# A transformer block on one core: the last down projection gets its weight remainders from adding transfers, and two more seven-product steps

## The chip, the cores and the metric

The kernel runs on one core of a Trainium2 chip, in one launch. The metric is the device time of a run in microseconds; for the kernel before it is the median of three runs. Beside it stands one profiled execution, whose trace gives start, duration and waits of every instruction.

## The reference

The reference is one block of a network with 256 rows (tokens) of width 2048, in float32: a first feed-forward part, a mixer of attention and convolution, and a second feed-forward part. Each reads the modulated norm of `x` and adds its gated result to `x`. The change concerns the last product of the second feed-forward part:

```python
def swiglu(h, w_gu, w_down):
    gu = jnp.einsum('bsd,df->bsf', h, w_gu)
    g, u = jnp.split(gu, 2, axis=-1)
    return jnp.einsum('bsf,fd->bsd', jax.nn.silu(g) * u, w_down)
...
h = modulate(rms_norm(x, ffn2_norm[l]), sh2, sc2)
x = x + FFN_RESIDUAL_WEIGHT * g2[:, None, :] * swiglu(h, ffn2_w_gu[l], ffn2_w_down[l])
```

Here `silu(g) * u` has 256 rows and 5632 columns, and `w_down` is 5632 x 2048.

## The kernel before, in words

**Split products.** TensorE multiplies in a rounded format (`F32R`). To keep float32's accuracy, each operand is split into its rounded part ("hi") and the remainder of the rounding ("lo"), and each product is made of three matmuls into one accumulator: hi by hi (L329), hi of the activations by lo of the weights (L333), and lo of the activations by hi of the weights (L334). This is `mm3`. The three are issued in this order; the second is the first to read a weight's remainder.

**Tiles of weights.** A weight tile is 1 MB, 128 partitions x 4 blocks of 512 columns. `w_tile` loads it from SP's queue into a buffer "raw" (L294; four buffers for the whole kernel), and for each half of it (two blocks, 128 x 1024) ScalarE casts the half to "whi" (L305; four buffers) and VectorE subtracts the cast from the raw half into "wlo" (L307; four buffers). The modulation's tiles (`w_ada`) also use "raw" buffers, but none is left after the first step of the stage below.

**The last down projection** is `down_strassen` (some 228 us at the end of the kernel). It makes the 2048 output columns in two pairs of 1024 (`np_` 0 and 1). In a pair it runs over 22 tiles (`c`), each of which holds 256 rows of `w_down` by 1024 columns, as a two by two matrix of blocks; the activations of the step are two by two as well (two halves of the 256 rows of `x`, two halves of the 256 contraction rows). Four accumulators `plain` hold the four output blocks. There are two kinds of steps:

- The ordinary step takes eight products (24 matmuls): for each half of the contraction and each output block, one product into that block's accumulator. Its tile comes from `w_tile`.
- The seven-product step, for the `c` in `SEVENS[np_]`, is a Strassen-Winograd step: 21 matmuls, on blocks, on sums of activation blocks and on differences of weight blocks, into `plain` and into four further accumulators `seven`, which are added to the outputs at the end of the pair. It loads "raw" (L542), casts and subtracts four groups (`split`, L512 and L513: b11, then b21 and b22, then t1 and t3, then t4 and t2), and makes the differences in place in "raw" on VectorE (L547, L549, L550). The sums of activations come from `sums_of` (L485 to L503: six operations on VectorE and a cast on ScalarE); those of the first `KEPT` = 6 seven-product steps of the first pair are kept for the second.

So a seven-product step takes four "whi" and four "wlo" buffers, an ordinary step two of each. Tiles 20 and 21 of the second pair are "held": their products are made last, output block by output block, so that each block can be finished and stored while the next is made.

**Order.** The kernel is written as a plain sequence; a scheduler places each engine's instructions in its queue, by their order in the program and by when it expects their operands, and adds the waits on data and on buffers that come free. An engine works through its queue in order.

Of the kernel before, what the change touches and what calls it, by code (L numbers as in the profile page):

```python
# [16 lines left out]
F32 = mybir.dt.float32  # L17
F32R = mybir.dt.float32r
# [4 lines left out]
ALU = mybir.AluOpType  # L23
AX = mybir.AxisListType

P = 128
# [27 lines left out]
TAPS_OUT = 12  # L54
WIDE = tuple(range(CK - 9, CK - 1))

SEVENS = ((3, 5, 9, 11, 13, 15, 17), (1, 3, 5, 7, 9, 11, 13, 15, 17))
KEPT = 6
CROSSBAR = {0: False, 96: True}
RMS_EPS = 1e-6  # L60
# [22 lines left out]
def block_kernel(ctx: ExitStack, tc: tile.TileContext, x_in, pos_in, w_ada, small, w_gu1, w_dn1,  # L83
                 w_in, w_out, w_gu2, w_dn2, out):
    nc = tc.nc
# [3 lines left out]
    rawp = ctx.enter_context(tc.tile_pool(name="rawp", bufs=4))  # L89
    whp = ctx.enter_context(tc.tile_pool(name="whp", bufs=4))  # L90
# [9 lines left out]
    def nm(s):  # L100
        uid[0] += 1
        return f"{s}_{uid[0]}"

    def blk(shape, dtype=F32):
        return blkp.tile(shape, dtype, tag="blk", name=nm("blk"))
# [38 lines left out]
    for i in range(4):  # L144
        pc = acc_tile()
        for j in range(4):
            k = 4 * i + j
# [138 lines left out]
    w_dma = [None]  # L286

    def w_tile(src, held=False, ks=(0, 4), small_raw=False):

        k0, n = ks[0], ks[1] - ks[0]  # L290
        src = src.rearrange("p (k n) -> p k n", k=4)
        if not small_raw:
            raw = rawp.tile([P, 4, 512], F32, tag="raw", name=nm("raw"))
            w_dma[0] = nc.sync.dma_start(out=raw[:, :n, :], in_=src[:, k0:k0 + n, :])  # L294
        views = {}
        for h in range(0, n, 2):
            m = min(2, n - h)
            if small_raw:
                part = blk([P, 2, 512])
                w_dma[0] = nc.sync.dma_start(out=part[:, :m, :], in_=src[:, k0 + h:k0 + h + m, :])  # L300
                rw = part[:, :m, :]
            else:
                rw = raw[:, h:h + m, :]
            hi = blk([P, 2, 512], F32R) if held else whp.tile([P, 2, 512], F32R, tag="whi", name=nm("whi"))
            nc.scalar.copy(out=hi[:, :m, :], in_=rw)  # L305
            lo = blk([P, 2, 512], F32R) if held else wlp.tile([P, 2, 512], F32R, tag="wlo", name=nm("wlo"))
            nc.vector.tensor_sub(out=lo[:, :m, :], in0=rw, in1=hi[:, :m, :].bitcast(F32))  # L307
            for j in range(m):
                views[k0 + h + j] = (hi[:, j, :], lo[:, j, :])
        return lambda j: views[j]  # L310

    def w_first(cs, held):
# [152 lines left out]
    def down_strassen(w_dn, aT, a_act, gate_of, evac_last, share, pend, finish):  # L465
# [13 lines left out]
        def sums_of(c):  # L479

            if c in kept:
                return kept[c]
            a = aT[c]
            full = tmp([P, 2, S])
            nc.vector.tensor_add(out=full, in0=a[:, 0].bitcast(F32), in1=a[:, 1].bitcast(F32))  # L485
            a11, a21, a12, a22 = full[:, 0, :P], full[:, 0, P:], full[:, 1, :P], full[:, 1, P:]
            q = tmp([P, 4, P])
            nc.vector.tensor_add(out=q[:, 0], in0=a21, in1=a22)
            nc.vector.tensor_sub(out=q[:, 1], in0=q[:, 0], in1=a11)
            nc.vector.tensor_sub(out=q[:, 2], in0=a11, in1=a21)  # L490
            nc.vector.tensor_sub(out=q[:, 3], in0=a12, in1=q[:, 1])
            keep = c in SEVENS[0][:KEPT]
            i = len(kept)
            if keep:
                if i < 2:
                    sp = in_c_bc[:, i]
                else:
                    sp = blk([P, 2, 4, P], F32R)
                hi, lo = sp[:, 0], sp[:, 1]
            else:  # L500
                hi, lo = tmp([P, 4, P], F32R), tmp([P, 4, P], F32R)
            nc.scalar.copy(out=hi, in_=q)
            nc.vector.tensor_sub(out=lo, in0=q, in1=hi.bitcast(F32))  # L503
            res = [(hi[:, i], lo[:, i]) for i in range(4)]
            if keep:
                kept[c] = res
            return res

        def split(src, n):
            hi = whp.tile([P, 2, 512], F32R, tag="whi", name=nm("whi"))  # L510
            lo = wlp.tile([P, 2, 512], F32R, tag="wlo", name=nm("wlo"))
            nc.scalar.copy(out=hi[:, :n, :], in_=src)  # L512
            nc.vector.tensor_sub(out=lo[:, :n, :], in0=src, in1=hi[:, :n, :].bitcast(F32))  # L513
            return [(hi[:, i, :], lo[:, i, :]) for i in range(n)]
# [4 lines left out]
        for np_ in range(2):  # L519
# [17 lines left out]
            for c in range(NCH):  # L537
                share()
                first, last = c == 0, c == NCH - 1
                if c in SEVENS[np_]:  # L540
                    raw = rawp.tile([P, 4, 512], F32, tag="raw", name=nm("raw"))
                    nc.sync.dma_start(out=raw, in_=w_dn[np_, c].rearrange("p (k n) -> p k n", k=4))  # L542
                    s1, s2, s3, s4 = sums_of(c)
                    (b11,) = split(raw[:, 0:1, :], 1)
                    b21, b22 = split(raw[:, 2:4, :], 2)

                    nc.vector.tensor_sub(out=raw[:, 0:2, :], in0=raw[:, 1:4:2, :], in1=raw[:, 0:2, :])  # L547
                    t1, t3 = split(raw[:, 0:2, :], 2)
                    nc.vector.tensor_sub(out=raw[:, 3, :], in0=raw[:, 3, :], in1=raw[:, 0, :])  # L549
                    nc.vector.tensor_sub(out=raw[:, 2, :], in0=raw[:, 2, :], in1=raw[:, 3, :])  # L550
                    t4, t2 = split(raw[:, 2:4, :], 2)
                    go, end = c == SEVENS[np_][0], c == SEVENS[np_][-1]
                    if go:
                        if np_ == 0:
                            seven = [acc_tile(), acc_tile(), tp_tile(), tp_tile()]
                        else:
                            seven = [acc_tile() for _ in range(4)]
                    mm3(seven[0], a_act(2 * c, 0), b11, go, end)
                    mm3(plain[0], a_act(2 * c + 1, 0), b21, False, False)
                    mm3(plain[1], s4, b22, False, False)  # L560
                    mm3(seven[1], s1, t1, go, end)
                    mm3(seven[3], s3, t3, go, end)
                    mm3(seven[2], s2, t2, go, end)
                    mm3(plain[2], a_act(2 * c + 1, 1), t4, False, False)
                    tick()
                    if end:

                        p1, p5, p6, p7 = seven
                        u = [tmp([P, 512]) for _ in range(5)]
                        last_pair = np_ == 1  # L570
                        nc.scalar.copy(out=u[0], in_=p1)
                        nc.vector.tensor_add(out=u[4], in0=p6, in1=u[0])

                        def step_1(u=u, p5=p5):
                            nc.vector.tensor_add(out=u[1], in0=p5, in1=u[4])

                        def step_2(u=u, p7=p7):
                            nc.vector.tensor_add(out=u[2], in0=p7, in1=u[4])

                        def step_3(u=u, p5=p5):  # L580
                            nc.vector.tensor_add(out=u[3], in0=p5, in1=u[2])

                        def add(i, u=u):

                            t, n, xs = place(i)
                            nc.vector.tensor_mul(out=u[i], in0=u[i], in1=gbc[n])
                            nc.vector.tensor_add(out=xs, in0=xs, in1=u[i])

                        if last_pair:
                            todo += [lambda: (step_1(), add(0), add(1)), lambda: (step_2(), step_3(), add(2)),  # L590
                                     lambda: add(3)]
                        else:
                            todo += [step_1, step_2, step_3]
                    continue
                w = w_tile(w_dn[np_, c])
                if np_ == 1 and c >= NCH - 2:
                    held.append((c, w))
                    if todo:
                        todo.pop(0)()
                    continue  # L600
                for k in range(2):
                    for i, (t, n) in enumerate(order):
                        mm3(plain[i], a_act(2 * c + k, t), w(2 * k + n), first and k == 0, last and k == 1)
                tick()
                if first and np_ == 0:
                    while pend:
                        finish(*pend.pop(0))
                    gbc = gate_of()
                if todo:
                    todo.pop(0)()  # L610
# [691 lines left out]
    for ci in range(10):  # L1302
        p0 = 1 if ci < HOLD else 0
        accs = first[ci][2] if ci < HOLD else [acc_tile() for _ in range(NT)]
        for pc in range(p0, 4):
# [3 lines left out]
            w = w_tile(w_in[ci, pc], ci == 0 and pc <= PRE)  # L1309
# [52 lines left out]
    for i, (n, pc) in enumerate([(n, pc) for pc in range(4) for n in range(3)]):  # L1362
        w = w_tile(w_out[n, pc])
# [106 lines left out]
```

## Time and profile before

| | |
|---|---|
| median of 3 runs | 1831.31 us (1829.83 to 1831.4) |
| the profiled execution | 1830.85 us, span of its trace 1829.0 us |
| mean granted TensorE clock | 0.998 |
| TensorE busy | 1800.7 us (98%) |
| VectorE busy | 1531.0 us (84%) |
| ScalarE busy | 1010.5 us (55%) |
| GpSimd busy | 28.3 us (2%) |
| read from DRAM | 492.37 MB, 270 GB/s over the span |
| queues of transfers | all data on SP's hardware queue |

How to read the profile's rows: PE is TensorE's matmuls, PEld its weight loads, DVE VectorE, ACT ScalarE, POOL GpSimd, SPq the queue from which SP issues transfers. In a group's row, "L307 DVE TENSOR_TENSOR wlo<-raw,whi 128x1024 ... x50 | 59.5, 1218 | 5.5 <-ACT whi L305 5.5" is the line, the engine, the operation, what it writes and reads, the count, then the busy time in us and the mean of one in ns, then how long the engine stood idle just before these instructions and what ended that idle time. In a row in order of time the first two numbers are start and duration in us; a matmul's duration overlaps the next one's. In a table of stretches stand the length, then for each engine the busy time and the count of instructions, then the granted clock of TensorE, the busy share of the transfer engines and what they moved. A transfer's row ends with the median time from its issue to its landing. A row of waits names who waited for whom, and then the sum, the times and the longest, in us.

### The profile page before, as it was taken

To read this page: it belongs to the slowest core of one execution; us is meant where nothing else is said; L and a number is where in the kernel's file an instruction comes from. 1 tells how busy PE (TensorE), PEld (TensorE's weight loads), DVE (VectorE), ACT (ScalarE), POOL (GpSimd) and SP (SyncE) were. 2 spreads that over 40 slices of the span, in tenths; PEclk is the share of its full clock that TensorE was granted. 3 is DMA by queue.
4 is the path that set the end of the run, shared out by engine and by line. 5 is a ranking of instruction groups with operands and counts; after the bars stand their busy time and mean duration, and the time that the engine had idled before them with its cause. 6 is when DMAs were issued, how large, how long until landed. Compare 5 with 4: busy or idle time off the path is not lost.

```text
span 1829.0 us, 21917 instructions
## 1 busy us (share of the span) xinstructions
PE 1800.7 (98%) x8111; PEld 1480.9 (81%) x8111; DVE 1531.0 (84%) x2040; ACT 1010.5 (55%) x1527; POOL 28.3 (2%) x29
## 2 busy tenths in 40 slices
PE   6999999999999999999999999999999999999998
PEld 5788888888888887788888787888888888878787
DVE  7889869999888787898999778878887865599897
ACT  7554344444444343566798655664755665555453
POOL 0000000000000000000110100000000000000000
PEclk9999999999999999999999999999999999999999
DMA  9987978889889998775544466889898966655552
GB/s 375 359 308 296 349 276 300 336 314 339 338 325 352 352 340 331 285 262 198 184 142 158 174 240 254 324 338 347 278 300 289 328 232 202 218 200 221 184 213 110
DMA packets 95962, 501.68 MB, mean 274 GB/s; under 512 B 31424, under 2 KB 31856, under 8 KB 38384
## 3 DMA queue, kind: packets, MB, share of 16 engines
q1 hardware_dynamic: 95856, 500.30, 74.7%
q8 instruction: 63, 1.03, 0.2%
q14 instruction: 43, 0.35, 0.1%
HBM read 492.37 MB, written 2.12 MB: 270 GB/s over the span
## 4 chain that ended last, share of the span: by engine, by line
PE 85%; DVE 8%; DMA 3%; ACT 3%; issue 2%; POOL 0%; SPq 0%; POOLq 0%; DVEq 0%; ACTq 0%
PE acc L333 27%; PE acc L334 27%; PE acc L329 27%; DVE wlo L307 2%; DVE wlo L513 1%; DMA raw<-in_w_ada_dram 1%; ACT whi L305 1%; DMA blk<-in_w_gu_dram 1%; PE acc L1137 1%; DVE raw L193 1%; DMA tmp<-tmp 1%; DVE blk L1029 1%; PE tp L851 1%; PE tp L333 1%; PE tp L334 1%
## 5 line engine op out<-in xcount | busy, mean ns | idle before, releaser
L333 PE MATMUL acc<-wlo,blk 128*128 128x512 f32 x2336 | 911.8, 390 | 6.3 <-DVE wlo L307 6.3
L329 PE MATMUL acc<-whi,blk 128*128 128x512 f32 x2339 | 909.5, 392 | 2.3 <-ACT blk L403 1.3
L334 PE MATMUL acc<-whi,blk 128*128 128x512 f32 x2336 | 910.7, 390 | 0.0
L305 ACT CAST whi<-raw 128x1024 fp32r<-128x1024 f32 (+1 forms) x577 | 592.4, 1044 | 475.5 <-PE acc L334 328.3
L307 DVE TENSOR_TENSOR wlo<-raw,whi 128x1024 fp32r<-128x1024 f32 (+1 forms) x577 | 686.5, 1210 | 180.3 <-ACT whi L305 179.5
L333 PEld LDWEIGHTS acc<-wlo,blk 128*128 128x128 f32 x2336 | 438.8, 188 | 101.4 <-DVE wlo L307 11.3
L329 PEld LDWEIGHTS acc<-whi,blk 128*128 128x128 f32 x2339 | 438.8, 188 | 94.6 <-ACT whi L305 2.7
L334 PEld LDWEIGHTS acc<-whi,blk 128*128 128x128 f32 x2336 | 438.5, 188 | 91.5 <-DVE blk L405 0.6
L193 DVE CUSTOM_DVE_ANT_0 raw<-raw,c_bc 128x2048 f32<-128x2048 f32 x142 | 324.2, 2285 | 10.3 <-DMA raw<-in_w_ada_dram 10.1
L512 ACT CAST whi<-raw 128x512 fp32r<-128x512 f32 (+1 forms) x64 | 60.5, 946 | 78.2 <-PE acc L334 27.5
L513 DVE TENSOR_TENSOR wlo<-raw,whi 128x512 fp32r<-128x512 f32 (+1 forms) x64 | 69.2, 1086 | 11.6 <-ACT whi L512 11.5
L666 ACT COPY blk<-acc 128x512 f32<-128x512 f32 x72 | 41.9, 589 | 62.6 <-PE acc L334 60.0
L1029 DVE SCALAR_TENSOR_TENSOR blk<-blk,cst,blk 128x245 f32<-128x245 f32 (+21 forms) x176 | 70.4, 455 | 0.6 <-ACT blk L1027 0.5
L830 DVE TENSOR_TENSOR blk<-acc,blk 128x512 f32<-128x512 f32 x88 | 56.7, 682 | 0.1
L845 ACT COPY tmp<-tmp 128x1024 uint16<-128x1024 uint16 x22 | 29.8, 1355 | 45.6 <-DMA tmp<-tmp 45.6
L831 ACT ACTIVATE blk<-blk 128x256 f32<-128x256 f32 x88 | 33.7, 413 | 19.6 <-DVE blk L830 19.4
L329 PE MATMUL acc<-blk,blk 128*128 128x512 f32 x104 | 40.8, 396 | 1.4 <-ACT blk L321 1.4
L333 PE MATMUL acc<-blk,blk 128*128 128x512 f32 x100 | 39.1, 391 | 0.8 <-DVE blk L307 0.8
L334 PE MATMUL acc<-blk,blk 128*128 128x512 f32 x100 | 39.0, 392 | 0.0
L351 DVE TENSOR_TENSOR blk<-tmp,blk 128x512 fp32r<-128x512 f32 x22 | 15.1, 688 | 22.3 <-ACT blk L350 22.3
L832 DVE TENSOR_TENSOR blk<-blk 128x256 f32<-128x256 f32 x88 | 33.8, 417 | 0.0
L307 DVE TENSOR_TENSOR blk<-raw,blk 128x1024 fp32r<-128x1024 f32 x24 | 28.9, 1220 | 2.0 <-ACT blk L305 2.0
(227 smaller groups left out, 1064.4 us busy)
## 6 DMA issues: line engine op xcount, KB each, us to landing
raw<-in_w_gu_dram SPq DMA_DIRECT2D x161, 1024.0 KB, 6.1
raw<-in_w_ada_dram SPq DMA_DIRECT2D x142, 1024.0 KB, 6.7
raw<-in_w_dn_dram SPq DMA_DIRECT2D x88, 1024.0 KB, 5.3
raw<-in_w_in_dram SPq DMA_DIRECT2D x40, 1024.0 KB, 4.8
raw<-in_w_out_dram SPq DMA_DIRECT2D x16, 1024.0 KB, 4.8
raw<-in_w_gu_dram SPq DMA_DIRECT2D x8, 768.0 KB, 6.3
blk<-in_w_gu_dram SPq DMA_DIRECT2D x10, 512.0 KB, 13.7
blk<-gate_line SPq DMA_DIRECT2D x6, 512.0 KB, 4.8
```

Source lines behind the costliest of these rows:

```text
L193: nc.vector.tensor_tensor_reduce(out=raw, in0=raw, in1=c_bc, scale=1.0, scalar=0.0, op0=ALU.mult, op1=ALU.add, accum_out=ada_cols[g][:, j ...
L305: nc.scalar.copy(out=hi[:, :m, :], in_=rw)
L307: nc.vector.tensor_sub(out=lo[:, :m, :], in0=rw, in1=hi[:, :m, :].bitcast(F32))
L329: nc.tensor.matmul(acc, ah, wh, start=start, stop=False)
L333: nc.tensor.matmul(acc, ah, wl, start=False, stop=False)
L334: return nc.tensor.matmul(acc, al, wh, start=False, stop=stop)
L512: nc.scalar.copy(out=hi[:, :n, :], in_=src)
L513: nc.vector.tensor_sub(out=lo[:, :n, :], in0=src, in1=hi[:, :n, :].bitcast(F32))
L666: last_part[0] = nc.scalar.copy(out=parts[c][:, t, :], in_=accs[t])
L830: nc.vector.tensor_add(out=p[:, t, :], in0=accs[t], in1=p[:, t, :])
L832: nc.vector.tensor_mul(out=p[:, t, 256:], in0=p[:, t, :256], in1=p[:, t, 256:])
L1029: nc.vector.scalar_tensor_tensor(out=y[:, d:], in0=u, scalar=w, in1=y[:, d:], op0=ALU.mult, op1=ALU.add)
```

## The change

The sets of seven-product steps become the odd `c` from 3 to 19 in the first pair (nine instead of seven: 7 and 19 are added) and the odd `c` from 1 to 17 in the second (as before). The remaining 26 ordinary tiles get their remainders in another way, by the new `w_tile_dma`: ScalarE casts each half to "whi" as before, then multiplies the cast by -1 into a second "raw" buffer, which now serves as the tile's "lo"; when both halves are there, a transfer issued from GpSimd's queue reads the weight tile from DRAM a second time and adds it onto this buffer. The remainder is then weight minus rounded weight, as before. VectorE has no part in it, and the "wlo" buffers are used by the seven-product steps alone. `w_tile` stays as it is for the other stages.

```diff
--- before.py
+++ after.py
@@ -54,7 +54,7 @@
 TAPS_OUT = 12
 WIDE = tuple(range(CK - 9, CK - 1))
 
-SEVENS = ((3, 5, 9, 11, 13, 15, 17), (1, 3, 5, 7, 9, 11, 13, 15, 17))
+SEVENS = (tuple(range(3, 20, 2)), tuple(range(1, 18, 2)))
 KEPT = 6
 CROSSBAR = {0: False, 96: True}
 RMS_EPS = 1e-6
@@ -307,6 +307,22 @@
             nc.vector.tensor_sub(out=lo[:, :m, :], in0=rw, in1=hi[:, :m, :].bitcast(F32))
             for j in range(m):
                 views[k0 + h + j] = (hi[:, j, :], lo[:, j, :])
+        return lambda j: views[j]
+
+    def w_tile_dma(src):
+
+        src = src.rearrange("p (k n) -> p k n", k=4)
+        raw = rawp.tile([P, 4, 512], F32, tag="raw", name=nm("raw"))
+        w_dma[0] = nc.sync.dma_start(out=raw, in_=src)
+        views = {}
+        lo = rawp.tile([P, 4, 512], F32R, tag="raw", name=nm("raw"))
+        for h in range(0, 4, 2):
+            hi = whp.tile([P, 2, 512], F32R, tag="whi", name=nm("whi"))
+            nc.scalar.copy(out=hi, in_=raw[:, h:h + 2, :])
+            nc.scalar.mul(lo[:, h:h + 2, :], hi.bitcast(F32), -1.0)
+            for j in range(2):
+                views[h + j] = (hi[:, j, :], lo[:, h + j, :])
+        nc.gpsimd.dma_start(out=lo, in_=src, accum_op=ALU.add)
         return lambda j: views[j]
 
     def w_first(cs, held):
@@ -592,7 +608,7 @@
                         else:
                             todo += [step_1, step_2, step_3]
                     continue
-                w = w_tile(w_dn[np_, c])
+                w = w_tile_dma(w_dn[np_, c])
                 if np_ == 1 and c >= NCH - 2:
                     held.append((c, w))
                     if todo:
```

## The prediction

> **What bounds the kernel now.** I read the page first: the span, the busy shares, and the chain that ended last.
>
> ```profile
> span 1829.0 us, 21917 instructions
> PE 1800.7 (98%) x8111; PEld 1480.9 (81%) x8111; DVE 1531.0 (84%) x2040; ACT 1010.5 (55%) x1527; POOL 28.3 (2%) x29
> PE 85%; DVE 8%; DMA 3%; ACT 3%; issue 2%; POOL 0%; SPq 0%; POOLq 0%; DVEq 0%; ACTq 0%
> ```
>
> TensorE is busy nearly all the time and carries the chain: an edit pays only if it takes matmuls away, and costs as soon as TensorE must wait. Then the table of stretches, for the last down projection alone, without its tail:
>
> ```profile
> core 0: us, PE busy (x) PEld busy (x) DVE busy (x) ACT busy (x) POOL busy (x), PEclk, DMA share, GB/s
> 1600.00:1780.00 180.00, 177.54 (x773) 143.75 (x772) 166.88 (x214) 97.23 (x108) 0.00 (x0) 1.00 0.55 202
> ```
>
> In these 180 us TensorE stands idle for only 2.46 us, VectorE is 93% busy, ScalarE 54%, the transfer engines 55%, and GpSimd does nothing. So VectorE has little room, but it does not yet hold TensorE up. The rest is read from one seven-product step and the ordinary step behind it, in order of time: TensorE's rows, then ScalarE's, VectorE's and the load queue's.
>
> ```profile
> 1755.66 0.39 PE L329 MATMUL acc<-whi,blk 128*128 128x512 f32 x1
> 1755.88 0.39 PE L333 MATMUL acc<-wlo,blk 128*128 128x512 f32 x1
> 1760.42 0.39 PE L329 MATMUL acc<-whi,blk 128*128 128x512 f32 x1
> 1760.64 0.39 PE L333 MATMUL acc<-wlo,blk 128*128 128x512 f32 x1
> 1756.19 1.05 ACT L512 CAST whi<-raw 128x1024 fp32r<-128x1024 f32 x1 [1.08 <-PE tp L334]
> 1757.15 2.00 ACT L305 CAST whi<-raw 128x1024 fp32r<-128x1024 f32 x2
> 1759.26 0.62 ACT L512 CAST whi<-raw 128x512 fp32r<-128x512 f32 x1
> 1758.42 2.35 DVE L307 TENSOR_TENSOR wlo<-raw,whi 128x1024 fp32r<-128x1024 f32 x2
> 1758.53 0.33 SPq L542 DMA_DIRECT2D raw<-in_w_dn_dram  x1
> ```
>
> The seven-product step starts at 1755.66 and the ordinary one at 1760.42. That is 4.76 us for 21 matmuls, 0.227 us each (a row's 0.39 us overlaps the next), and so 5.44 us for an ordinary step of 24. The reader is to see how late the ordinary tile is rounded: its two casts run from 1757.15 to 1759.15, while the step before it is on TensorE, because they reuse two of only four "whi" buffers, and these come free as that step's first matmuls read them. The remainders follow at once on VectorE (1758.42 to 1760.77), and TensorE asks for the first at 1760.64. There is no whole step of lead: from the last cast to the first use of a remainder are 1.5 us.
>
> **The change, part by part.** *Two more seven-product steps.* In the first pair c = 7 and c = 19 change kind: 2 x 3 = 6 matmuls fewer, 6 x 0.227 = 1.4 us off TensorE. In the second pair the set stays. With six sums kept as before, now those of 3 to 13, the second pair still makes three anew (1, 15, 17). Each converted step adds the sums and the splitting, by these groups of the stage:
>
> ```profile
> L513 DVE TENSOR_TENSOR wlo<-raw,whi 128x1024 fp32r<-128x1024 f32 (+1 forms) x63 | 68.5, 1093 | 9.3 <-ACT whi L512 9.2
> L512 ACT CAST whi<-raw 128x1024 fp32r<-128x1024 f32 (+1 forms) x63 | 59.9, 951 | 78.2 <-PE acc L334 27.5 <-DVE raw L547 17.7 <-DVE raw L550 14.0
> L307 DVE TENSOR_TENSOR wlo<-raw,whi 128x1024 fp32r<-128x1024 f32 x50 | 59.5, 1218 | 5.5 <-ACT whi L305 5.5
> L305 ACT CAST whi<-raw 128x1024 fp32r<-128x1024 f32 x50 | 51.1, 1050 | 19.2 <-PE acc L334 10.4 <-PE tp L334 7.0 <-DVE tmp L490 1.7
> L547 DVE TENSOR_TENSOR raw<-raw 128x1024 f32<-128x1024 f32 x16 | 19.5, 1221 | 0.2
> L550 DVE TENSOR_TENSOR raw<-raw 128x512 f32<-128x512 f32 x16 | 11.0, 687 | 0.2
> L485 DVE TENSOR_TENSOR tmp<-blk 128x512 f32<-128x512 f32 x10 | 6.8, 681 | 0.0
> L488 DVE TENSOR_TENSOR tmp<-tmp 128x128 f32<-128x128 f32 x10 | 2.9, 285 | 0.1
> ```
>
> Splitting costs VectorE 4 x 1.09 + 1.22 + 2 x 0.69 = 7.0 us, the sums 0.68 + 4 x 0.285 + about 0.68 = 2.5 us: 9.5 us a step, 19 us for two. ScalarE gets 4 x 0.95 + 0.62 = 4.4 us each, less the two casts of the ordinary step.
>
> *Remainders off VectorE.* There were 28 ordinary steps, each with two subtractions of 1.22 us: all are gone, -68 us. With the 19 us above VectorE falls by 49 us and can't be a bound any more. Its idle time is worth nothing beyond the 2.46 us that TensorE waits.
>
> *Negations onto ScalarE.* 26 ordinary tiles x 2, priced like the cast beside them (1.05 us, same shape and engine): +55 us on an engine that is 54% busy. It stays under 90%, so the sum is covered. Their place is not: ScalarE works in order, so the negations lie behind the casts on the way to the remainder.
>
> *The adding transfer, and the wait that it brings.* The remainder now exists when a transfer, issued on GpSimd's queue behind both negations, has added the weights from DRAM onto them. The queue was empty in this stage (0.00 above), so nothing is queued behind it. On TensorE everything is: the second matmul of the step reads the remainder, and the engine goes in order. Call T the time from the last negation to the landing. No row shows an adding transfer. The nearest, for transfers in this stage and for its loads over the whole run:
>
> ```profile
> raw<-in_w_dn_dram SPq DMA_DIRECT2D x39, 1024.0 KB, 4.9
> out_dram<-xall SPq DMA_DIRECT2D x7, 256.0 KB, 2.1
> DMA to landing us min/median/max: 4.7/5.3/9.7
> blk<-in_w_gu_dram SPq DMA_DIRECT2D x10, 512.0 KB, 13.7
> ```
>
> Lower end: a plain 1 MB load, 4.9 us. Upper end: the slowest median on the page, 13.7 us. Between: from 256 KB at 2.1 to 1 MB at 4.9 are 3.65 us per MB on a fixed 1.2; an add must fetch the weights and the tile it adds to, two megabytes, so 1.2 + 7.3 = 8.5 us (estimate from these rows). I take 8.5, which also lies near the slowest 1 MB load (9.7): the add meets the loads of the next tiles on the same engines.
>
> The Trainium skill (DMA: Bandwidth & Descriptors, section on the anatomy of one DMA on the GpSimd path) fits 2.0 us plus bytes over 436 GB/s to such transfers, so 4.4 us for a tile, as an estimate; by it the sum below would be about 100 us instead of 226. That fit is of copies, and no run shows an add yet.
>
> **The sum.** Let the seven-product step begin at S. ScalarE's order is: the step's own last cast at S + 0.5, then the casts of the ordinary tile from S + 1.5 (row 1757.15), now with two negations: 4 x 1.05, so issue at S + 5.6. The remainder lands at S + 5.6 + T. TensorE reaches the ordinary step at S + 4.8 and can go on for four matmuls, one for each accumulator, which need no remainder; rows show that such matmuls are put ahead:
>
> ```profile
> 1738.47 0.39 PE L329 MATMUL tp<-whi,blk 128*128 128x512 f32 x1
> 1738.95 0.74 PE L329 MATMUL acc<-whi,blk 128*128 128x512 f32 x2
> 1739.53 0.40 PE L333 MATMUL acc<-wlo,in_c_bc 128*128 128x512 f32 x1
> ```
>
> So it needs the remainder at S + 5.7 and waits T - 0.1, say T. Nothing covers this: the next steps' tiles need "whi" buffers that the waiting step holds, so no work is done ahead and every pair waits anew. Without the four matmuls ahead it would be T + 0.7; with three products of the next step put into the gap, T - 0.7: the bounds.
>
> *What the wait does to the clock.* The start of the kernel shows a long wait of TensorE: three stretches of the granted clock, with two matmuls in the third.
>
> ```profile
> 7.44:10.86 3.42, 0.00 (x0) 0.00 (x0) 2.50 (x5) 1.44 (x4) 0.89 (x1) 1.00 1.01 402
> 10.86:14.27 3.41, 1.11 (x4) 0.71 (x4) 3.30 (x10) 1.50 (x3) 0.56 (x1) 0.50 1.06 387
> 14.27:17.68 3.41, 3.06 (x7) 2.40 (x8) 2.53 (x5) 2.43 (x5) 0.00 (x0) 0.50 0.99 381
> 15.21 0.63 PE L333 MATMUL acc<-wlo,blk 128*128 128x512 f32 x1
> 15.64 0.63 PE L334 MATMUL acc<-whi,blk 128*128 128x512 f32 x1
> ```
>
> After a stretch of 3.4 us without a matmul the clock is 0.50, for two such stretches, until one of them (3.06 us busy) has been nearly full. Matmuls then start every 0.43 us instead of 0.227. A wait of 8.5 us holds such an idle stretch wherever it falls; one of 4.9 us does in (4.9 - 3.4) / 3.4 = 44% of cases. Back at work, TensorE is slow for the rest of a stretch and then a full one, 3.4 to 6.8 us, 5.1 in the mean: 12 matmuls where 22.5 would have run, 2.4 us lost each time. The Trainium skill (TensorE: Matmul & The Clock Gate, Part 1) states this as a rule: half rate after an idle window of about 3.4 us, full rate after a busy one. The trace agrees, with its 3.41 us stretches.
>
> *The terms.* Eighteen ordinary steps follow a seven-product step (4 to 20 even in the first pair, 2 to 18 in the second): 18 x (8.5 + 2.4) = 196 us. Of the others, the first step has its casts three half steps ahead (8.2 us of lead + 0.9 - 5.3 of casts and negations): T - 3.8 = 4.7. Three stand behind two ordinary steps (2, then 0 and 20 of the second pair); their remainder's buffer, now one of the four "raw" buffers, comes free one step ahead, 5.4 + 0.9 - 3.5: T - 2.8 = 5.7 each, 17.1. The held pair at the end waits once more for tile 21, about 4. Steps 1, 21 and 19 are ready in the wait of the step before. These five shorter waits lower the clock in about half the cases, 6 us. Together 196 + 4.7 + 17.1 + 4 + 6 - 1.4 = 226 us. The profiled execution took 1830.85 us (span 1829.0), 0.46 under the median shown: 1830.85 + 226 = **2057 us**.
>
> *The "raw" buffers.* An ordinary tile now takes two of four, so the load of a seven-product step waits until the ordinary step two before has ended. That is one step and the wait ahead, 4.8 + 5.4 + 8.5 us for a load of 4.9: covered. Without the wait it would still be 10.2 us for 4.9 and the split. The 26 adds move 26 or, read twice, 52 MB in a stage with 45% of the transfer engines free, which moreover gets longer: covered.
>
> **The rivals.** *A, the add costs no more than a plain load.* T = 4.9: 18 x (4.9 + 0.44 x 2.4) + 1.1 + 6.3 + 4 - 1.4 = +117, 1948 us. With the products put ahead (18 x 0.7 less, and the clock falling in 23% of the waits) it is +95, 1926. For it: 45% of the transfer engines are idle. Against: two megabytes, and loads in between. The Trainium skill's fit (4.4 us) stands nearest to this one.
>
> *B, the add is slow.* T = 13.7: 18 x 16.1 + 9.9 + 32.7 + 4 + 10 - 1.4 = +345, 2176 us. For it: the page has transfers that need that long when many are under way, and here two loads and an add share a pair. Against: the loads of this stage have a median of 4.9.
>
> *C, the other side: hidden.* If the compiler's order gives the ordinary tile its casts a full step earlier, the add lands before TensorE asks. It decides when the casts start about T = 8.5 us sooner than in the row at 1757.15, which four "whi" buffers don't allow as the waits on released buffers show:
>
> ```profile
> ACT whi L512 <- PE acc L334: 27.5, 22, 4.6
> ACT whi L305 <- PE acc L334: 10.4, 8, 1.7
> ```
>
> Then only -1.4 us is left, 1829.5, and if the freed VectorE ends TensorE's waits as well (2.46), 1827.0: at the edge of what counts as faster.
>
> **How the numbers follow.** Forecast (T from 6 to 11, by the same terms +156 to +284, so 1987 to 2115): 0.52. A 0.2, B 0.2, C 0.06, something unforeseen on the fast side 0.02. The number is the forecast's at T = 8.5, 2057. The range reaches from A's lower bound, 1926, to 2130, which leaves out most of B and all of C. About 0.2% (3.7 us) is what a measurement of this kernel can tell from no change: C falls mostly inside it. Slower 0.92, same 0.05, faster 0.03.
>
> **What would show it.** In the changed kernel's table of stretches TensorE should be idle for some 40% of the last stage and its granted clock near 0.8 there, with VectorE under 50%. The waits should name GpSimd's adding transfer as what TensorE's L333 waits for, some 22 times, about 8.5 us each; the issue row of that transfer gives T. Matmuls that start 0.43 us apart should stand behind each wait, and a pair of steps should take 10.2 + T + 2.4, near 21 us. The converted steps should show as 18 seven-product steps with 3 matmuls fewer than before, twice. I am wrong if the wait is not there (casts earlier than the buffers seemed to allow), if TensorE finds other matmuls for the gap, or if T is far from 8.5, which shifts the time by about 22 us per microsecond.

## The result, and the profile after

The changed kernel takes 2044.71 us (median of 4 runs, 2041.77 to 2046.09) beside 1831.36 us for the kernel before on the same chip: a ratio of 1.1164, 95% interval 1.1144 to 1.1183. The profiled execution took 2041.77 us, 210.9 more than that of before; the lines below are from it. The page first, with the same three lines as of before:

```profile
span 2039.9 us, 22057 instructions
PE 1861.8 (91%) x8105; PEld 1514.6 (74%) x8105; DVE 1488.6 (73%) x2010; ACT 1070.6 (52%) x1585; POOL 51.4 (3%) x55
PE 71%; issue 19%; DMA 4%; DVE 4%; ACT 2%; POOL 0%; SPq 0%; POOLq 0%; DVEq 0%; ACTq 0%
```

TensorE was 98% busy and is 91% busy, with six matmuls fewer. ("issue" in the chain is time in which the profile shows nothing that was waited for.) The last stage alone, in the table of stretches:

```profile
1600.00:1990.00 390.00, 258.78 (x884) 194.75 (x883) 156.34 (x213) 158.51 (x172) 17.63 (x20) 0.78 0.58 164
```

TensorE stands idle for a third of it, at a granted clock of 0.78; VectorE has fallen from 93% to 40%, and the transfer engines are at 58%: nothing is near its limit any more. The time lies in waits, and the waits of the stage name one:

```profile
PE acc L349 <- DMA raw<-in_w_dn_dram: 132.4, 22, 9.2
ACT whi L528 <- PE tp L350: 78.3, 10, 11.8
```

(L349 is now the matmul by the weights' remainder; L333 before.) 22 times, 6.0 us each, it waits for the transfer that adds the weights onto the negated parts. The row of that transfer on the page, and its queue's:

```profile
raw<-in_w_dn_dram POOLq DMA_DIRECT2D x26, 1024.0 KB, 7.9
q0 software_dynamic: 3744, 27.26, 6.9%
```

It lands 7.9 us after its issue. One pair of steps in order of time, ScalarE, GpSimd's queue and TensorE:

```profile
1907.24 1.06 ACT L321 CAST whi<-raw 128x1024 fp32r<-128x1024 f32 x1 [2.26 <-PE tp L350]
1910.36 1.06 ACT L322 ACTIVATE raw<-whi 128x1024 fp32r<-128x1024 f32 x1
1892.03 0.88 POOL L325 DMA_DIRECT2D raw<-in_w_dn_dram  x1 [19.19 <-DMA raw<-in_w_dn_dram]
1911.83 0.90 POOL L325 DMA_DIRECT2D raw<-in_w_dn_dram  x1 [18.92 <-ACT raw L322]
1911.12 0.61 PE L345 MATMUL acc<-whi,blk 128*128 128x512 f32 x2
1911.58 0.61 PE L345 MATMUL tp<-whi,blk 128*128 128x512 f32 x2
1912.48 0.49 PE L345 MATMUL acc<-whi,blk 128*128 128x512 f32 x1 [0.29 <-ACT whi L528]
1919.62 0.80 PE L349 MATMUL acc<-raw,blk 128*128 128x512 f32 x1 [5.68 <-DMA raw<-in_w_dn_dram]
```

The last negation ends at 1911.42 and the transfer is issued at 1911.83. TensorE has come to the ordinary step at 1911.12, makes its four products that need no remainder, then three of the next step, and stands until 1919.62. From one issue to the next are 19.8 us; 45 matmuls at 0.227 us are 10.2. Behind the wait the clock is down, as two starts 0.43 us apart show:

```profile
1901.14 0.63 PE L349 MATMUL acc<-raw,blk 128*128 128x512 f32 x1
1901.56 0.63 PE L350 MATMUL acc<-whi,blk 128*128 128x512 f32 x1
```

### The profile page after: what moved, and what is told of

Its sections match the earlier page's. It is cut to its first block, busy times and chain, and to the rows that moved or that the text cites. A ratio compares the mean times of both kernels' runs of the same rounds, so it can differ in the third digit from the quotient of the medians.

```text
span 2039.9 us, 22057 instructions
## 1 busy us (share of the span) xinstructions
PE 1861.8 (91%) x8105; PEld 1514.6 (74%) x8105; DVE 1488.6 (73%) x2010; ACT 1070.6 (52%) x1585; POOL 51.4 (3%) x55
## 3 DMA queue, kind: packets, MB, share of 16 engines
q0 software_dynamic: 3744, 27.26, 6.9%
## 4 chain that ended last, share of the span: by engine, by line
PE 71%; issue 19%; DMA 4%; DVE 4%; ACT 2%; POOL 0%; SPq 0%; POOLq 0%; DVEq 0%; ACTq 0%
PE acc L349 23%; PE acc L350 23%; PE acc L345 23%; DMA raw<-in_w_dn_dram 2%; DVE wlo L307 1%; DMA blk<-in_w_gu_dram 1%; PE acc L1153 1%; ACT whi L305 1%; DVE raw L193 0%; DVE blk L1045 0%; PE tp L867 0%; PE tp L410 0%; DMA raw<-in_w_in_dram 0%; DMA blk<-in_w_ada_dram 0%; DVE blk L307 0%
## 5 line engine op out<-in xcount | busy, mean ns | idle before, releaser
L349 PE MATMUL acc<-wlo,blk 128*128 128x512 f32 x2170 | 849.1, 391 | 10.9 <-DVE wlo L529 6.0
L305 ACT CAST whi<-raw 128x1024 fp32r<-128x1024 f32 x521 | 536.9, 1044 | 468.6 <-PE acc L350 338.4
L307 DVE TENSOR_TENSOR wlo<-raw,whi 128x1024 fp32r<-128x1024 f32 x521 | 621.1, 1211 | 171.9 <-ACT whi L305 170.7
L345 PEld LDWEIGHTS acc<-whi,blk 128*128 128x128 f32 x2329 | 442.6, 190 | 111.3 <-ACT whi L528 17.3
L350 PEld LDWEIGHTS acc<-whi,blk 128*128 128x128 f32 x2326 | 450.0, 193 | 94.0 <-DVE blk L421 0.7
L349 PEld LDWEIGHTS acc<-wlo,blk 128*128 128x128 f32 x2170 | 407.7, 188 | 102.9 <-DVE wlo L529 11.4
L193 DVE CUSTOM_DVE_ANT_0 raw<-raw,c_bc 128x2048 f32<-128x2048 f32 x142 | 324.4, 2286 | 10.7 <-DMA raw<-in_w_ada_dram 10.0
L349 PE MATMUL acc<-raw,blk 128*128 128x512 f32 x156 | 86.0, 551 | 138.4 <-DMA raw<-in_w_dn_dram 138.4
L349 PEld LDWEIGHTS acc<-raw,blk 128*128 128x128 f32 x156 | 41.5, 266 | 158.3 <-DMA raw<-in_w_dn_dram 113.5
L321 ACT CAST whi<-raw 128x1024 fp32r<-128x1024 f32 x52 | 54.0, 1046 | 70.0 <-PE acc L350 38.6
L322 ACT ACTIVATE raw<-whi 128x1024 fp32r<-128x1024 f32 x52 | 54.7, 1058 | 1.2
L325 POOL DMA_DIRECT2D raw<-in_w_dn_dram x26 | 23.1, 888 | 885.3 <-ACT raw L322 822.1
L345 PE MATMUL acc<-blk,blk 128*128 128x512 f32 x104 | 40.8, 395 | 0.6 <-ACT blk L337 0.6
```

What stands on the lines that cost most here:

```text
L193: nc.vector.tensor_tensor_reduce(out=raw, in0=raw, in1=c_bc, scale=1.0, scalar=0.0, op0=ALU.mult, op1=ALU.add, accum_out=ada_cols[g][:, j ...
L321: nc.scalar.copy(out=hi, in_=raw[:, h:h + 2, :])
L322: nc.scalar.mul(lo[:, h:h + 2, :], hi.bitcast(F32), -1.0)
L345: nc.tensor.matmul(acc, ah, wh, start=start, stop=False)
L349: nc.tensor.matmul(acc, ah, wl, start=False, stop=False)
L350: return nc.tensor.matmul(acc, al, wh, start=False, stop=stop)
```

## The experiments

All were compared with the kernel before on the same chip; times are medians. Where a time is set against the changed kernel's 2044.7 us, the kernel before took 1831.4 us beside that one, and 1829.5 to 1831.2 beside the experiments. My theory was the prediction's: the chain of cast, negation and landing stands ahead of TensorE without any lead, and each wait lowers the clock. The rivals were the two further seven-product steps, the bytes moved, and GpSimd's path.

**1. The seven-product steps alone.**

```diff
-                w = w_tile_dma(w_dn[np_, c])
+                w = w_tile(w_dn[np_, c])
```

> Nine seven-product steps in either pair, but the ordinary tiles' remainders are subtracted on VectorE as before. Theory (the adding transfer's landing is the whole loss): 6 matmuls of 0.227 us fewer, 1.4 us: about 1830 us, no change that can be measured. Rival (the two further seven-product steps load VectorE too much, 2 x (9.5 - 2.4) = 14 us more on an engine 93% busy): up to 10 us slower, 1841.

Measured: 1833.73 us beside 1829.67, ratio 1.0021 (1.0012 to 1.0030). The theory's 1.4 us gain did not come; there is a loss of 4 us, within the rival's "up to 10". The stretch quoted in the prediction, for this kernel, and one of its waits:

```profile
1600.00:1780.00 180.00, 175.60 (x750) 138.51 (x750) 175.85 (x234) 98.27 (x112) 0.00 (x0) 1.00 0.55 204
ACT whi L528 <- DVE raw L563: 39.7, 13, 4.6
```

VectorE is 98% busy, ScalarE's casts wait for VectorE's differences for 39.7 us (17.7 before), and TensorE's idle time has grown from 2.46 to 4.40 us. So the steps carry some 4 of the 211 us at most, and only while VectorE makes all the remainders.

**2. The adding transfers alone.**

```diff
-SEVENS = (tuple(range(3, 20, 2)), tuple(range(1, 18, 2)))
+SEVENS = ((3, 5, 9, 11, 13, 15, 17), (1, 3, 5, 7, 9, 11, 13, 15, 17))
```

> The sets of seven-product steps as before, the remainders by adding transfers. Theory: 16 waits behind seven-product steps instead of 18, but three more ordinary steps that stand behind two others; 16 x 9.6 + 6 x 6.5 + 20 = about 213 us over before, so 2035 to 2050, as the whole change. Rival (the seven-product steps carry the loss): near 1831.

Measured: 2045.42 us, ratio 1.1174 (1.1157 to 1.1191), in the expected range and the same as for the whole change. The loss comes with the new way to the remainder.

**3. A copy in place of the add.**

```diff
-        nc.gpsimd.dma_start(out=lo, in_=src, accum_op=ALU.add)
+        nc.gpsimd.dma_start(out=lo, in_=src)
```

> The changed kernel, but the transfers on GpSimd's queue copy the weights over the negated parts instead of adding them: the remainders are left wrong, everything else stands. Theory (the add moves two megabytes, and that is what makes 7.9 us of landing): the copy lands in 4.9 to 5.7 us like a plain load, some 2.4 us less in about 20 waits and fewer falls of the clock: 1965 to 1990. Rival 1 (the landing is the price of the GpSimd path and the adding is free): still 7.9 us and 2040 to 2047. Rival 2, the Trainium skill's fit for copies on this path (DMA: Bandwidth & Descriptors), an estimate of 4.4 us: about 1955.

Measured: 1980.3 us, in the expected range and 64 less than the changed kernel, though still 151 over the kernel before. The row of the transfer and its queue's, and a stretch and TensorE's waits:

```profile
raw<-in_w_dn_dram POOLq DMA_DIRECT2D x24, 1024.0 KB, 5.3
q0 software_dynamic: 3744, 27.26, 3.8%
1600.00:1800.00 200.00, 151.15 (x523) 114.00 (x523) 99.95 (x152) 95.46 (x106) 7.04 (x13) 0.81 0.53 195
PE acc L349 <- DMA raw<-in_w_dn_dram: 77.1, 21, 6.9
```

The same bytes, by the row, land after 5.3 us instead of 7.9 and keep the transfer engines busy for about half the time: 3.8% of 1980.5 us are 2.9 us for each of 26 tiles, 6.9% of 2039.9 are 5.4. An add costs the engines nearly two copies, and rival 1, by which the adding is free, is out. The Trainium skill's fit for transfers on this path (DMA: Bandwidth & Descriptors, the anatomy of one DMA) gives 4.4 us, as an estimate; the copies here landed in 5.3.

The waits are only 3.7 us in the mean now, and yet the granted clock is 0.81. By the trace's record it falls in 19 of TensorE's 20 idle gaps of over 2 us, or at most 1 us behind them, and 11 of these gaps are no longer than 2.3 to 3.3 us.

**4. and 5. Work in the wait.** Matmuls by zeros, which change no sum, between the four first products and the first by a remainder.

```diff
+                        for z in range(ZEROS):
+                            i = z % 4
+                            nc.tensor.matmul(plain[i], zero, w(order[i][1])[0], start=False, stop=False)
```

> The changed kernel, with 20 matmuls more in each ordinary step but the last two: their stationary operand is all zeros, they are placed after the step's four first products and before the first that reads a remainder, 4.5 us of work that changes no sum. To make room for the zeros, five sums are kept instead of six. Theory (each wait also lowers the clock for some 5 us, 2.2 us lost): the idle stretch falls from 5.7 to under 2 us, the clock stays at 1.00, and the kernel gets faster by 18 to 22 x 2.2 us although it does more: 1995 to 2010. Rival (the lower clock costs nothing because the time is spent waiting anyway): 2040 to 2047.

Measured with 20 of them: 2040.8 us, ratio to before 1.1153 (1.1137 to 1.1170). That is in the rival's range: the expected gain did not show. The row of the wait and two behind it say why:

```profile
1917.42 0.50 PE L629 MATMUL acc<-raw,blk 128*128 128x512 f32 x1 [3.37 <-DMA raw<-in_w_dn_dram]
1919.06 0.63 PE L629 MATMUL tp<-raw,blk 128*128 128x512 f32 x1
1919.49 0.63 PE L630 MATMUL tp<-whi,blk 128*128 128x512 f32 x1
```

3.4 us of idle time were left, and behind it the matmuls still slowed down, from 0.23 to 0.43 us apart. So there were too few zeros to tell the two apart. The next kernel has more of them, and only in the steps with a long wait.

> As the kernel with zeros in the wait, but 32 such matmuls (7.3 us) and only in the 18 ordinary steps behind a seven-product step. With 20 the wait still held about 3.3 us of idle time and the clock still fell for 1.3 to 2.2 us, so that the test was blunt. Theory (a long wait costs its lowered clock as well): under 1.5 us of idle time is left, the granted clock of the stage stays above 0.95, and the kernel is 18 x 1.7 to 2.2 us faster than the changed one with 576 matmuls more: 2000 to 2018 us. Rival (the clock costs nothing): 2040 to 2047 or, with the zeros in the way, more.

Measured: 2024.99 us, ratio 1.1057 (1.1039 to 1.1075), which is 20 us faster than the changed kernel with 576 matmuls more. The stretch and the two rows between which the loss is read:

```profile
1600.00:1990.00 390.00, 354.79 (x1501) 286.25 (x1502) 168.22 (x231) 164.44 (x180) 19.42 (x22) 0.97 0.66 175
1873.39 0.47 PE L629 MATMUL acc<-raw,blk 128*128 128x512 f32 x1 [0.78 <-DMA raw<-in_w_dn_dram]
1882.81 0.61 PE L623 MATMUL acc<-whi,blk 128*128 128x512 f32 x2
```

The clock stays at 0.97, and from the landing to the next ordinary step are 9.42 us for 41 matmuls, 0.23 each. In the changed kernel the same way, 1900.12 to 1911.12, takes 11.0 us for 38: 2.4 us more than at 0.227. So a long wait costs its lowered clock too, and the rival is out: with more work this kernel is faster. The gain is smaller than the 27 us that the slow end of the expected range stands for. GpSimd's issues lie 18.6 us apart in the mean (1634.09 to 1783.45 for eight pairs, 1846.87 to 1957.85 for six) instead of 19.9, so only 1.3 of the 2.4 us come back: the zeros take the place of the three products that had been put into the gap (0.7 us), and the transfer lands after 8.1 us instead of 7.9.

**6. One adding transfer for each half.**

```diff
+            nc.gpsimd.dma_start(out=lo[:, h:h + 2, :], in_=src[:, h:h + 2, :], accum_op=ALU.add)
...
-        nc.gpsimd.dma_start(out=lo, in_=src, accum_op=ALU.add)
```

> The changed kernel with two adding transfers for each ordinary tile, one for each half, issued as soon as that half is negated. Theory (TensorE waits for the chain cast, negation, landing): the first half is issued 2 us sooner and moves half the bytes, 1.2 + 3.65 = 4.9 us by the rows used before: it lands near S + 8.9 where TensorE stands at S + 5.7 to 6.4. Waits of about 3 us instead of 5.7 plus 0.7 of filling, and the clock falls less: 4 us lost in a pair instead of 9.6, 1895 to 1940 us. Rival (the number of bytes added in the stage or GpSimd's descriptor work bounds it): 2030 or more.

Measured: 2000.54 us, 44 less than the changed kernel, where I had expected 105 to 150. Two rows, of the transfer and of ScalarE:

```profile
raw<-in_w_dn_dram POOLq DMA_DIRECT2D x48, 512.0 KB, 7.8
1880.58 2.00 ACT L321 CAST whi<-raw 128x1024 fp32r<-128x1024 f32 x2
1882.48 2.00 ACT L322 ACTIVATE raw<-whi 128x1024 fp32r<-128x1024 f32 x2
```

I had worked out 4.9 us from sizes alone. The row's 7.8 us mix the two halves of a tile; as far as the trace tells them apart, from 1626 us on the first half lands after 7.1 us in the median (5.3 to 8.9), and the second, behind it on the same engines, after 8.3. So even the quickest half needs more than 4.9. That the others are slower because they share the engines with the loads of the next tiles is likely, but no run here shows it by itself. And in some pairs, as in the two rows of ScalarE, the order has both casts first and both negations after them, so that nothing is issued earlier. My way of scaling T by bytes is refuted for halves that follow each other.

**7. The remainders' products last**, in the held tiles too.

```diff
-                        mm3(plain[i], a_act(2 * c + k, t), w(2 * k + n), first and k == 0, last and k == 1)
+                    nc.tensor.matmul(plain[i], ah, wh, start=first and k == 0, stop=False)
+                    nc.tensor.matmul(plain[i], al, wh, start=False, stop=False)
...
+                for k, i, t, n in prods:
...
+                    nc.tensor.matmul(plain[i], ah, wl, start=False, stop=last and k == 1)
```

> The changed kernel with an ordinary step's eight products by remainders moved behind its other sixteen matmuls. Theory: 3.6 us of work stand ahead of the first use of a remainder instead of 0.9, so each long wait is 2.7 us shorter: 18 x 2.7 and some 10 us at the other steps, 1975 to 1995 us. Rival (transfers in a row bound the pair, whatever TensorE does in the gap): 2040 to 2047.

Measured: 1984.75 us, ratio 1.0842 (1.0824 to 1.0860), in the expected range and 60 less than the changed kernel, with the same transfers (8.0 us to landing). In this kernel, what TensorE can do ahead of its first use of a remainder counts in full.

**8. Casts in buffers of their own.**

```diff
-KEPT = 6
+KEPT = 2
...
-            hi = whp.tile([P, 2, 512], F32R, tag="whi", name=nm("whi"))
+            hi = blk([P, 2, 512], F32R)
```

> The changed kernel with the ordinary tiles' casts in four buffers of their own, taken from the buffers of kept sums (two sums kept instead of six, so that VectorE and ScalarE make four more in the second pair). One adding transfer for each tile as in the changed kernel. Theory (the four whi buffers shared with the seven-product steps take the lead away): the casts can start when the raw tile is loaded; now the raw buffers set the time, the transfer is issued near S - 10.2 + 12 and lands 4 us after TensorE asks for it: 1910 to 1970 us. Rival (the lead is not what matters; the add is too slow for a pair of steps however early it could start): 2030 or more.

Measured: 1948.63 us, ratio 1.0643 (1.0623 to 1.0663), in the range and 96 us less than the changed kernel, although its transfers land later. Two rows of its transfers; then what the ordinary tiles' casts wait for, two rows of the changed kernel and two of this one:

```profile
raw<-in_w_dn_dram POOLq DMA_DIRECT2D x24, 1024.0 KB, 9.9
raw<-in_w_dn_dram SPq DMA_DIRECT2D x41, 1024.0 KB, 6.9
ACT whi L321 <- PE acc L350: 31.6, 12, 8.8
ACT whi L321 <- PE tp L350: 28.1, 10, 9.2
ACT blk L321 <- DMA raw<-in_w_dn_dram: 53.7, 17, 11.8
ACT blk L321 <- PE acc L350: 3.5, 3, 1.8
```

In the changed kernel the casts wait for TensorE to give "whi" buffers free; here they wait for the load of their own tile. So the four shared "whi" buffers did hold the lead back. With it the adds and loads now run side by side: 9.9 and 6.9 us instead of 7.9 and 5.2.

**9. to 11. What bounds it then.** Lead with halves, lead with the remainders' products last, and lead with copies.

> Both: casts in buffers of their own, and one adding transfer for each half. Theory: the first half now lands before TensorE asks for it, and only short waits are left: 1830 to 1850 us. Rival (bytes or descriptor work bound the stage): as slow as with the halves alone, 1895 or more.

> The kernel with casts in buffers of their own (lead), and the products by remainders last in an ordinary step. Theory A (what is left is a ring of waits through TensorE: buffer free, load, cast, negation, landing): TensorE asks 2.7 us later, so the pair shrinks by that, 18 x 2.7 and some clock: 1870 to 1900 us. Theory B (the transfer engines are full: two loads of 8 x 0.31 us an engine and an add of 8 x 0.63 are 10 us in a pair of 10.2, and they can't be packed closer than in lead): 1935 to 1955 us.

> The kernel with casts in buffers of their own (lead), with a copy in place of the add, so that the remainders are left wrong. A pair's transfers then take 7.5 us of an engine instead of 10, and the landing is 2.6 us sooner. Theory A (ring of waits): 18 x 2.7 us and some clock less than 1949: 1870 to 1900 us. Theory B (engines full): as much or more, 1850 to 1880. It tells little between A and B by itself; with the run before it: if only this one gains, it is B.

Measured: 1964.85 us with halves (ratio 1.0751, 1.0699 to 1.0803), 1969.5 with the products last (1.0752, 1.0732 to 1.0771), and 1904.14 with copies (1.0395, 1.0366 to 1.0424). With halves the theory missed and the rival's range holds; with the products last both theories missed, since it is slower than either had it. Both kernels are slower than lead alone. With copies it is 45 us faster than lead, and still slower than either theory had it. Neither a smaller transfer nor a later use helps any more; only the cheaper transfer does. By the rule set beforehand that speaks for theory B, the transfers' engines, but not for engines that are simply full: in the stage's first 180 us they are busy for 81% in lead and for 72% with the products last. The rows of that kernel point to the buffers:

```profile
ACT whi L528 <- DMA raw<-in_w_dn_dram: 89.3, 16, 11.5
raw<-in_w_dn_dram SPq DMA_DIRECT2D x41, 1024.0 KB, 7.8
1869.98 0.33 SPq L558 DMA_DIRECT2D raw<-in_w_dn_dram  x1
1878.50 1.57 ACT L528 CAST whi<-raw 128x512 fp32r<-128x512 f32 x2 [11.33 <-DMA raw<-in_w_dn_dram]
```

The seven-product step's own tile is loaded late, when an ordinary tile's remainder has left a "raw" buffer, and then lands in 8 us beside another load and an add. (TensorE's last matmul by the remainder ends at 1869.90, and the load is issued at 1869.98.) That this is what binds is read from these rows, not shown by a run: no kernel with more "raw" buffers was run, so the share of buffers and engines stays open.

**12. Another way to unload VectorE.** No adding transfers; the second half's remainder on GpSimd.

```diff
-            nc.vector.tensor_sub(out=lo, in0=raw[:, h:h + 2, :], in1=hi.bitcast(F32))
+            eng = nc.gpsimd if h else nc.vector
+            eng.tensor_sub(out=lo, in0=raw[:, h:h + 2, :], in1=hi.bitcast(F32))
```

> Another way to unload VectorE: no adding transfers; nine seven-product steps in either pair, and the second half of each ordinary tile's remainder is subtracted on GpSimd, the first on VectorE. Theory (with the subtractions on VectorE the two further steps cost 4 us since VectorE is full; 26 x 1.22 us less on it gives that back): 1827 to 1830 us, at the edge of faster than before. Rival (GpSimd is slow at it, or holds VectorE up at the memory's port): 1835 or more.

Measured: 1864.24 us, ratio 1.0181 (1.0166 to 1.0196): the rival's range. Three lines of the remainder's tile tell both halves of it, minimum, median and maximum in ns:

```profile
L529 DVE TENSOR_TENSOR wlo<-raw,whi x72: 677/1218/2766, 1601.4 to 1826.6; 128x1024 fp32r<-128x1024 f32 x54, 128x512 fp32r<-128x512 f32 x18
L323 DVE TENSOR_TENSOR wlo<-raw,whi x23: 1208/1219/2681, 1596.4 to 1839.9; 128x1024 fp32r<-128x1024 f32 x23
L323 POOL TENSOR_TENSOR wlo<-raw,whi x23: 2439/2627/10650, 1597.4 to 1836.0; 128x1024 fp32r<-128x1024 f32 x23
```

GpSimd takes at least 2.4 us for what VectorE does in 1.2, at worst 10.7, and VectorE's own subtractions stretch to 2.8 (at most 1.23 in the kernel before, from 1600 to 1780 us). The Trainium skill (SBUF — State Buffer, who interferes with whom) states that a VectorE operation with two inputs in SBUF contends with a GpSimd one that reads it; the stretched operations agree. No version here beats the kernel before.

## Why the prediction was right, point by point

It said 2057 us, by +226; +211 was measured on the profiled execution and +213 by the medians. The mechanism was right, and one large term carries the number. That it came within some 7% owes something to luck: the long waits were 21 us too dear, the other steps 5 too cheap.

- *What bounds, and where the wait goes.* Right: TensorE's chain, and the new wait at the first product by a remainder. Experiment 2 puts the whole loss on the new way to the remainder, 3 puts 64 us of it on the adding, 7 and 8 show that their price is set by what TensorE can do ahead of its first use of a remainder and by the "whi" buffers, as argued.
- *T.* 8.5 us taken, 7.9 measured from issue to landing and 0.4 more from the last negation to the issue: 8.3. That an add costs about twice a copy was right for the engines (experiment 3: 5.4 us of their time against 2.9); why it does, no run here shows, for the queue's row counts the same 27.26 MB for both. The rest was partly luck. The line through two rows, one of them a store of 256 KB, failed for the halves: 4.9 us against 7.1 for the first of them. And the add hardly meets the loads of the next tiles, which was an argument for 8.5: in the changed kernel the pair's loads are issued 4.4 us ahead of it or more (1907.05 and 1907.47, by SP's rows, against 1911.83) and land after 5.2. Where adds and loads do meet, in lead, an add needs 9.9.
- *The long waits.* 18 x (8.5 + 2.4) = 196 us was the term. Issues lie 19.9 us apart in the mean of a run of pairs (1628.28 to 1767.84 for seven of them, 1853.27 to 1972.57 for six), 9.7 over 10.2: 175 us, if all 18 cost that. The 21 us too much are the three products of the next step that the order puts into the gap, the bound that I had named and not taken (18 x 0.7 = 13), and T (18 x 0.2), with a rest.
- *The clock.* 2.4 us a wait, and 2.4 in the pair worked out above. The stage's clock was to be near 0.8 and is 0.78. The condition, a whole stretch of 3.4 us without a matmul, was too narrow, which a wait as long as these does not bring out: the shorter gaps of experiment 3 lowered the clock all the same, and in experiment 4 so did 11 of 15 gaps of 3.1 to 3.5 us. So "44% of cases" at 4.9 us was too low, and with it rival A's price: +117 at 4.9 us, where the copies at 5.3 us cost +151. What the condition is stays open.
- *The other steps.* 32 us were given to them; 211 + 1.4 - 175 = 37 are left, if the 1.4 us of the six matmuls are counted as won.
- *The engines' sums.* VectorE's busy time fell by 42 us (49 forecast), ScalarE's rose by 60 (by the terms given, 55 + 8.8 - 4.2 = 60).
- *What would show it.* The table of stretches has the idle share at 34% (some 40% was said), VectorE at 40% (under 50%) and 22 waits as said, but of 6.0 us and not 8.5: the four products and the three of the next step run while the transfer is under way, and I had counted the landing as if it were all waiting.
- *The two further steps, at -1.4 us.* "VectorE does not yet hold TensorE up" was true of the kernel before, but left no room for 14 us more: by themselves the steps lost 4 us (experiment 1). In the changed kernel VectorE is unloaded, and no effect of them can be told (2044.7 us with, 2045.4 without them).
- *"45% of the transfer engines free", as cover for the adds.* This holds only because the stage got longer. At the old pace a pair of 10.2 us would carry 55% of loads, 5.6 us, and 5.4 us of adds: more than there is. Had the lead been there, this would have been the next bound, and experiments 9 to 11 ran into its neighbourhood. Rival C, the hidden transfer at 1827 to 1830, had on these sums no room for its gain, whatever the order.

## What to carry to other kernels

Before work is moved from a full engine to an idle resource, count the time from its last input to its result and look for the buffers that give this time: here a remainder of 2 x 1.2 us on VectorE, ready just in time, became 2 us of negation and 8 us of transfer, and no buffer was free to start earlier. A wait of TensorE can cost more than itself, since the clock falls with it (here 2.4 us for 6.0 of waiting); work that must be done anyway (here the other sixteen matmuls) belongs into the gap first. And an engine at 93% may have no room for two further steps (here 14 us of work more cost 4), even if hardly anything waits for it yet.

## What the runs showed of the hardware that I had not expected

An adding transfer of 1 MB keeps the transfer engines busy for 5.4 us a tile, a copy for 2.9. Split into two of 512 KB, it gains little for the first use: the first half lands after 7.1 us in the median, the whole after 7.9. Idle gaps of TensorE of 2.3 to 3.5 us, with matmuls on both sides, were mostly enough to lower the clock; with the zeros, behind gaps of 3.1 and 3.4 us, it fell only after the work had begun again (starts 0.43 us apart from 1.2 and 1.6 us on). GpSimd's subtraction of 128x1024 took 2.4 to 10.7 us beside VectorE's, which went from 1.2 to as much as 2.8 us.
